# Two-layer hybrid decoder trunk: weight sums by adding transfers, and two plain blocks per feed-forward part instead of three, the second's low weight parts on GpSimd

## The chip, the cores and the metric

The kernel runs on one core of a Trainium2 chip. The core has a matrix engine (TensorE, PE in the rows; its weight loads are listed as PEld), VectorE (DVE), ScalarE (ACT), GpSimd (POOL) and SyncE (SP), which issues most transfers. Each engine works through its own queue in order and waits there for semaphores of the others. The metric is the device time of one execution in microseconds.

## The reference

Two layers on 528 tokens (16 meta tokens and 512 real ones) of width 1024, all in float32:

```python
xn = rmsnorm(h, attn_norm_g)
proj = jnp.einsum('bld,dc->blc', xn, w_in)
...
mix = jnp.concatenate([fox_out, ret_out], axis=-1)
h = h + jnp.einsum('blc,cd->bld', mix, w_out)
hn = rmsnorm(h, ffn_norm_g)
ff = jax.nn.silu(jnp.einsum('bld,df->blf', hn, w_gate)) * jnp.einsum('bld,df->blf', hn, w_up)
return h + jnp.einsum('blf,fd->bld', ff, w_down)
```

`fox_out` is causal attention of 8 heads with a forget gate, `ret_out` chunked retention of 4 heads with a group norm. The hidden width of the feed-forward part is 2816. A last norm follows, and the 16 meta tokens are dropped. The change touches the feed-forward part alone.

## The kernel before

**Numbers.** Each float32 operand of a product is split into a high and a low part (a cast on ACT, a subtraction that leaves the rest), and a product is three matmuls: high weights by high x, high by low, low by high. The split of weights is made in `convert` for plain jobs (cast at line 180, low part at 183, on GpSimd where the job has its `pool` flag, in pieces of 128 columns, else on VectorE in pieces of 512) and in `splits` for the others (cast at 888, low part at 889, always VectorE). The split of x and of activations is `split` (131 and 132).

**The feed-forward part** of a layer works on 22 blocks of 128 hidden columns, in the six rounds of `ROUNDS`. Layer 0 has 528 columns of x, in two halves of 264; layer 1 computes only the 512 real ones. x lies in eight tiles of 128 rows, k = 0 to 7.

**Plain blocks.** The first `PLAIN` blocks take gate and up as two dense products (`dense_steps`, matmuls at 206). Gate goes through `g_done` (833 or 836: scaling, then silu), up through `u_done` (844, 845, and the split of the activation into `ah`, `al`).

**Units.** The other blocks are made by `Unit`: seven products of half the depth and half the columns take the place of eight, at the price of sums of weights and of x. A unit's order on TensorE is `head` (8 chunks on plain x), `middle` (12 chunks, from `w2` and half of `w3`, on forms of x), `tail` (8 chunks), each chunk three matmuls (line 900) of 264 or 256 columns. Its weights are four jobs: `make1` splits the gate block a; `make2` makes s, whose second half is the sum of the halves of the up block b (934) and whose first half is that less a's first half (935); `make3` makes a's first half less b's first half (941); `make4` subtracts s from a's second half (947). a lies in a buffer `raw`, b in `fraw`, s in one of two buffers `S`, which the forms of x share; high and low parts lie in rings `whi`, `wlo`, `fwhi`, `fwlo` of two.

**Forms of x.** `x_forms(k)`, for k = 0 to 3, makes four sums of x's halves (861 to 865), splits them into `th` and `tl` for all units of the layer, and is placed among the steps of the plain blocks. The first unit's `middle` is the first to read them, k = 0 to 3 in turn.

**End of a unit.** `keep` copies partial results into `e` on ACT (966), `done` combines them (976 to 984) and splits the activation. The down products of a round (1035) run as `fills` between the units of the next round; a unit that has no such fill leaves its `tail` to `tails`, which is put behind the next unit's `head`.

**What sets the order.** TensorE's order is the order of the steps. The other engines' queues are ordered by a scheduler that places an instruction by its own estimate of when its inputs and buffers are there; pools give a buffer to the next tile when the last reader of the old one is done. Weights are loaded by SyncE (924 in `Unit.load`, two transfers per unit).

Of the kernel before, what the change touches and what calls it, by code (L numbers as in the profile page):

```python
# [20 lines left out]
DEPTH = 2  # L21
# [6 lines left out]
PLAIN = 3  # L28
# [11 lines left out]
def hybrid_kernel(ctx, tc, x_t, w_in, w_fl, w_out, w_gate, w_up, w_down, vecs, b_fg, rope, decay, mask, ident, out_t):  # L40
# [772 lines left out]
    def ffn(l, st, real, last):  # L813
# [40 lines left out]
        def x_forms(k):  # L854
            def go():
                if k == 0:
                    st["t"] = [[fft(f"t{p}{i}", shape=(128, 2, 4, w)) for p in "hl"] for i in range(2)]
                s = fft("S", F32, (128, 6, w), 2)
                a, b = ((h[k][:, c0:c1], h[HB + k][:, c0:c1]) for c0, c1 in HC)
                g0, g1 = vcol(V_FFN + l * NK + k), vcol(V_FFN + l * NK + HB + k)  # L860
                nc.scalar.activation(s[:, 0:2], two(h[k]), AF.Copy, scale=g0)
                nc.vector.tensor_sub(s[:, 2], s[:, 1], s[:, 0])
                for i in range(2):
                    nc.vector.scalar_tensor_tensor(s[:, 3 + i], b[1], g1, s[:, 1 + i], ALU.mult, ALU.subtract)
                nc.vector.scalar_tensor_tensor(s[:, 5], a[1], g1, s[:, 4], ALU.mult, ALU.subtract)
                th, tl = (t[:, k % 2] for t in st["t"][k // 2])
                split(th, tl, s[:, 2:6])
# [39 lines left out]
        class Unit:  # L907
# [12 lines left out]
            def load(self):  # L920
                if "a" not in self.t:
                    for n, src, pool, tag, bufs in (("a", w_gate, wp, "raw", 3), ("b", w_up, phase["ffn"], "fraw", 2)):
                        self.t[n] = pool.tile([128, NK, 128], F32, name=tag, tag=tag, bufs=bufs)
                        nc.sync.dma_start(self.t[n], src[l, self.f])

# [5 lines left out]
            def make2(self, hi, lo):  # L931
                a, b = self.t["a"], self.t["b"]
                s = self.t["s"] = fft("S", F32, (128, NK, 128), 2)
                nc.vector.tensor_add(s[:, HB:NK], b[:, 0:HB], b[:, HB:NK])
                nc.vector.tensor_sub(s[:, 0:HB], s[:, HB:NK], a[:, 0:HB])
# [3 lines left out]
            def make3(self, hi, lo):  # L939
                a, b = self.t["a"], self.t["b"]  # L940
                nc.vector.tensor_sub(b[:, 0:HB], a[:, 0:HB], b[:, 0:HB])
                splits(hi, lo, b)


            def make4(self, hi, lo):
                a, s = self.t["a"], self.t["s"]
                nc.vector.tensor_sub(a[:, HB:NK], a[:, HB:NK], s[:, 0:HB])
# [24 lines left out]
            def done(self):  # L972
# [8 lines left out]
                nc.vector.scalar_tensor_tensor(u[:, c], sg[:, c], RSC, st["R"][:, c], ALU.mult, ALU.mult)  # L981
# [67 lines left out]
        for r, (f0, f1) in enumerate(ROUNDS):  # L1049
            for f in range(f0, f1):  # L1050
                if f < PLAIN:
                    steps += dense_steps(w_gate[l, f], [(0, xs, NK, QC, g_done(f) if f else held.append)], banks=f == 1)
                    steps += dense_steps(w_up[l, f], [(0, xs, NK, QC, u_done(f))])
# [188 lines left out]

    gf = const.tile([128, NK], F32, name="gf")
# [180 lines left out]
```

## Time and profile before

| | us |
|---|---|
| median of 3 runs (lowest to highest) | 1272.61 (1271.99 to 1272.77) |
| the profiled execution | 1272.43 |
| its span | 1270.6 |
| PE busy in the span | 1253.3 |
| DVE busy | 998.6 |
| ACT busy | 687.3 |
| POOL busy | 266.9 |
| TensorE clock granted | 0.999 |

The span runs from the first to the last instruction that the profile shows; the execution takes a little more. The profile is of one execution. In rows of groups, a line of the kernel is followed by the engine, the operation, what it writes and reads, the count, the busy time in us and the mean of one in ns. In rows of the timeline, the first number is the start in us from the span's start and the second the duration; consecutive instructions of an engine overlap a little, so a start less the one before it tells how long an instruction holds its engine up. In layer 0 the first matmul of block 0 starts at 286.53, of block 1 at 298.92, of block 2 at 310.50 and of the first unit at 322.07; in layer 1 they start at 913.00, 925.41, 936.49 and 947.53.

### The profile page before, as it was taken

Reading aid. Unit: us, or ns where it says so; the run is one execution under the profiler, and the core shown is the slowest. Engines: PE = TensorE matmul, PEld = TensorE weight load, DVE = VectorE, ACT = ScalarE, POOL = GpSimd, SP = SyncE. Lnnn points to the kernel's source line nnn. Section 1 sums busy time; section 2 is a strip of 40 time slices with the busy share of each in tenths; the row PEclk is TensorE's granted clock in tenths of the full one; section 3 lists DMA queues with packets and bytes.
Section 4 is the critical chain, followed back from the end, with each engine's and each line's share of the span. In section 5 each row is a group of like instructions: output and inputs, shape, how many; then the busy total and the mean of one; then the engine's idle time right before and its main releaser. Section 6 shows DMA issues by size and latency. Waiting matters only on the chain.

```text
span 1270.6 us, 23600 instructions
## 1 busy us (share of the span) xinstructions
PE 1253.3 (99%) x9263; PEld 1195.1 (94%) x9263; DVE 998.6 (79%) x1852; ACT 687.3 (54%) x1246; POOL 266.9 (21%) x527
## 2 busy tenths in 40 slices
PE   9999999999999999999999999999999999999997
PEld 8899999999999999999998989998789999999996
DVE  8878756779888888887786877567899888888866
ACT  7666545676444444444465665456764444444444
POOL 3455545410000000000025546454100000000000
PEclk9999999999999999999999999999999999999999
DMA  6322222123233333332323232222233333333321
GB/s 217 95 71 89 87 81 83 60 68 129 92 96 100 100 100 100 100 100 84 107 70 117 61 101 83 78 90 67 100 96 121 100 100 100 100 100 100 102 81 67
DMA packets 45680, 120.57 MB, mean 95 GB/s; under 512 B 5360, under 2 KB 12272, under 8 KB 45568
## 3 DMA queue, kind: packets, MB, share of 16 engines
q1 hardware_dynamic: 45136, 118.77, 29.7%
q8 instruction: 73, 1.20, 0.4%
q14 instruction: 39, 0.32, 0.1%
q10 hardware_dynamic: 432, 0.29, 0.1%
HBM read 116.91 MB, written 2.13 MB: 94 GB/s over the span
## 4 chain that ended last, share of the span: by engine, by line
PE 93%; DVE 2%; ACT 2%; DMA 2%; issue 0%; SPq 0%; DVEq 0%; ACTq 0%
PE psd L206 29%; PE psa L900 19%; PE psd L1035 14%; PE psd L900 13%; PE psa L206 5%; PE psa L1035 4%; PE psa L407 2%; PE psa L582 2%; PE psa L497 2%; PE psa L749 1%; PE psa L719 1%; DMA bc<-cdr 1%; DMA h<-x_t 0%; DMA cdr<-z 0%; PE psa L279 0%
## 5 line engine op out<-in xcount | busy, mean ns | idle before, releaser
L183 POOL TENSOR_TENSOR wlo<-raw,whi 128x128 fp32r<-128x128 f32 x504 | 261.4, 554 | 270.0 <-ACT whi L180 250.0
L206 PE MATMUL psd<-xh,whi 128*128 128x264 f32 (+1 forms) x792 | 195.4, 314 | 0.2 <-ACT whi L180 0.2
L206 PE MATMUL psd<-xl,whi 128*128 128x264 f32 (+1 forms) x792 | 186.0, 302 | 0.5 <-DVE xl L309 0.4
L206 PE MATMUL psd<-xh,wlo 128*128 128x264 f32 (+1 forms) x792 | 186.4, 303 | 0.0
L206 PEld LDWEIGHTS psd<-xh,whi 128*128 128x128 f32 x792 | 128.0, 189 | 5.2 <-ACT whi L180 0.9
L206 PEld LDWEIGHTS psd<-xh,wlo 128*128 128x128 f32 x792 | 126.8, 188 | 6.3 <-DVE wlo L183 0.6
L206 PEld LDWEIGHTS psd<-xl,whi 128*128 128x128 f32 x792 | 127.4, 188 | 5.0 <-DVE xl L309 1.2
L180 ACT CAST whi<-raw 128x512 fp32r<-128x512 f32 (+1 forms) x168 | 98.4, 613 | 49.3 <-PE psd L206 36.4
L888 ACT CAST whi<-raw 128x1024 fp32r<-128x1024 f32 (+2 forms) x62 | 54.8, 885 | 51.3 <-PE psd L900 39.9
L888 ACT CAST fwhi<-raw 128x1024 fp32r<-128x1024 f32 (+2 forms) x62 | 55.6, 897 | 47.5 <-PE psd L900 40.0
L1135 POOL TENSOR_TENSOR th<-th,e 128x544 f32<-128x544 f32 x1 | 1.4, 1370 | 359.1 <-DVE e L1155 359.1
L85 POOL MEMSET kl<- 64x528 f32 x2 | 1.1, 534 | 345.4 <-PE psa L900 345.4
L889 DVE TENSOR_TENSOR wlo<-raw,whi 128x1024 fp32r<-128x1024 f32 (+2 forms) x62 | 62.9, 1015 | 12.8 <-ACT whi L888 12.7
L889 DVE TENSOR_TENSOR fwlo<-raw,fwhi 128x1024 fp32r<-128x1024 f32 (+2 forms) x62 | 64.0, 1032 | 10.5 <-ACT fwhi L888 10.1
L900 PE MATMUL psa<-th,whi 128*128 128x264 f32 (+1 forms) x232 | 65.4, 282 | 0.0
L900 PE MATMUL psa<-th,wlo 128*128 128x264 f32 (+1 forms) x232 | 65.4, 282 | 0.0
L900 PE MATMUL psa<-tl,whi 128*128 128x264 f32 (+1 forms) x232 | 65.3, 282 | 0.0
L900 PE MATMUL psa<-th,fwhi 128*128 128x264 f32 (+1 forms) x224 | 63.4, 283 | 0.0
L900 PE MATMUL psa<-tl,fwhi 128*128 128x264 f32 (+1 forms) x224 | 63.3, 283 | 0.0
L900 PE MATMUL psa<-th,fwlo 128*128 128x264 f32 (+1 forms) x224 | 63.3, 282 | 0.0
L517 ACT ACTIVATE pd<-pd,nmax 128x144 f32<-128x144 f32 (+1 forms) x64 | 36.9, 576 | 43.8 <-DVE nmax L504 31.8
L966 ACT COPY e<-psa 128x264 f32<-128x264 f32 (+1 forms) x114 | 42.9, 376 | 28.4 <-PE psa L900 24.1
(343 smaller groups left out, 4053.5 us busy)
## 6 DMA issues: line engine op xcount, KB each, us to landing
raw<-w_in SPq DMA_DIRECT2D x54, 512.0 KB, 3.4
raw<-w_gate SPq DMA_DIRECT2D x44, 512.0 KB, 3.8
fraw<-w_up SPq DMA_DIRECT2D x38, 512.0 KB, 3.5
raw<-w_down SPq DMA_DIRECT2D x64, 256.0 KB, 2.8
raw<-w_out SPq DMA_DIRECT2D x16, 512.0 KB, 3.4
raw<-w_down SPq DMA_DIRECT2D x32, 192.0 KB, 2.5
bc<-cdr SPq DMA_DIRECT2D x16, 264.0 KB, 3.5
raw<-w_up SPq DMA_DIRECT2D x6, 512.0 KB, 3.5
```

What stands on the lines that cost most here:

```text
L180: pin(nc.scalar.copy(hi, job["raw"][:, c0:c1]), pinned)
L183: pin(sub(lo[:, i:i + wide], job["raw"][:, c0 + i:c0 + i + wide], hi[:, i:i + wide].bitcast(F32)), pinned)
L206: nc.tensor.matmul(ps[1][b][:, 0:c1 - c0], w[:, wk, :], x[:, c0:c1], start=(k == 0 and i == 0), stop=(k == n - 1 and i == 2))
L407: nc.tensor.transpose(ps[:, 128 * j:128 * j + 128], src[:, o:o + 128], idt)
L497: nc.tensor.matmul(sc[0:nq, 0:c1 - c0], st["q"][s][:, q0:q0 + nq], kk[:, c0:c1], start=(i == 0), stop=(i == 1))
L517: nc.scalar.activation(pr, pr, AF.Exp, bias=nmax[0:nq], scale=-1.0, accum_out=rsum)
L582: nc.tensor.matmul(po[:, c0:SEQ], v[:, j, :], pp[:, j, META + c0:T], start=(j == 0 and i == 0), stop=(j == 4 and i == 1))
L888: nc.scalar.copy(hi, src)
L889: nc.vector.tensor_sub(lo, src, hi.bitcast(F32))
L900: nc.tensor.matmul(bank()[:, 0:b.shape[-1]], a[:, o + k, :], b, start=(fresh and k == 0 and i == 0), stop=(k == n - 1 and i == 2), skip_gr ...
L966: nc.scalar.copy(self.t["e"][:, i], self.t["x"][:, 0:w])
L1035: nc.tensor.matmul(v[:, 0:c1 - c0], a[:, s * n + k, :], b[:, c0:c1], start=(k == 0 and i == 0), stop=(k == n - 1 and i == 2))
```

## The change

Block 2 of each layer becomes a unit, and block 1 remains plain with its low weight parts on GpSimd (`f > 0` is the `pool` flag). The first unit then has no down product of an earlier round beside it, so its tail goes behind the next unit's head. For every unit the sum of the halves of b is made by transfers: SyncE loads the first half into s, a transfer from GpSimd's queue adds the second half to it; another adds a's first half to b's first half, again from memory. The sums at 934 and 941 go. Because a transfer can only add, some signs are turned round: the forms of x use gains of opposite sign (`ngf`, made once), two subtractions of weights become additions, and `done` scales by `-RSC`. The signs cancel in the end.

```diff
--- before.py
+++ after.py
@@ -25,7 +25,7 @@
 DFF = 2816
 NF = DFF // 128
 ROUNDS = ((0, 3), (3, 7), (7, 11), (11, 15), (15, 19), (19, 22))
-PLAIN = 3
+PLAIN = 2
 HB = NK // 2
 EPS = 1e-6
 NBLK = SEQ // 128
@@ -858,11 +858,12 @@
                 s = fft("S", F32, (128, 6, w), 2)
                 a, b = ((h[k][:, c0:c1], h[HB + k][:, c0:c1]) for c0, c1 in HC)
                 g0, g1 = vcol(V_FFN + l * NK + k), vcol(V_FFN + l * NK + HB + k)
+                n1 = ngf[:, l * HB + k:l * HB + k + 1]
                 nc.scalar.activation(s[:, 0:2], two(h[k]), AF.Copy, scale=g0)
-                nc.vector.tensor_sub(s[:, 2], s[:, 1], s[:, 0])
-                for i in range(2):
-                    nc.vector.scalar_tensor_tensor(s[:, 3 + i], b[1], g1, s[:, 1 + i], ALU.mult, ALU.subtract)
-                nc.vector.scalar_tensor_tensor(s[:, 5], a[1], g1, s[:, 4], ALU.mult, ALU.subtract)
+                nc.vector.tensor_sub(s[:, 2], s[:, 0], s[:, 1])
+                nc.vector.scalar_tensor_tensor(s[:, 3], b[1], g1, s[:, 1], ALU.mult, ALU.subtract)
+                nc.vector.scalar_tensor_tensor(s[:, 4], b[1], n1, s[:, 2], ALU.mult, ALU.subtract)
+                nc.vector.scalar_tensor_tensor(s[:, 5], a[1], n1, s[:, 4], ALU.mult, ALU.subtract)
                 th, tl = (t[:, k % 2] for t in st["t"][k // 2])
                 split(th, tl, s[:, 2:6])
             return go
@@ -922,6 +923,10 @@
                     for n, src, pool, tag, bufs in (("a", w_gate, wp, "raw", 3), ("b", w_up, phase["ffn"], "fraw", 2)):
                         self.t[n] = pool.tile([128, NK, 128], F32, name=tag, tag=tag, bufs=bufs)
                         nc.sync.dma_start(self.t[n], src[l, self.f])
+                    s = self.t["s"] = fft("S", F32, (128, NK, 128), 2)
+                    nc.sync.dma_start(s[:, HB:NK], w_up[l, self.f, :, 0:HB])
+                    nc.gpsimd.dma_start(s[:, HB:NK], w_up[l, self.f, :, HB:NK], accum_op=ALU.add)
+                    nc.gpsimd.dma_start(self.t["b"][:, 0:HB], w_gate[l, self.f, :, 0:HB], accum_op=ALU.add)
 
 
             def make1(self, hi, lo):
@@ -929,22 +934,18 @@
 
 
             def make2(self, hi, lo):
-                a, b = self.t["a"], self.t["b"]
-                s = self.t["s"] = fft("S", F32, (128, NK, 128), 2)
-                nc.vector.tensor_add(s[:, HB:NK], b[:, 0:HB], b[:, HB:NK])
-                nc.vector.tensor_sub(s[:, 0:HB], s[:, HB:NK], a[:, 0:HB])
+                a, s = self.t["a"], self.t["s"]
+                nc.vector.tensor_add(s[:, 0:HB], s[:, HB:NK], a[:, 0:HB])
                 splits(hi, lo, s)
 
 
             def make3(self, hi, lo):
-                a, b = self.t["a"], self.t["b"]
-                nc.vector.tensor_sub(b[:, 0:HB], a[:, 0:HB], b[:, 0:HB])
-                splits(hi, lo, b)
+                splits(hi, lo, self.t["b"])
 
 
             def make4(self, hi, lo):
                 a, s = self.t["a"], self.t["s"]
-                nc.vector.tensor_sub(a[:, HB:NK], a[:, HB:NK], s[:, 0:HB])
+                nc.vector.tensor_add(a[:, HB:NK], a[:, HB:NK], s[:, 0:HB])
                 splits(hi, lo, a[:, HB:NK])
 
             def bank(self, n):
@@ -978,7 +979,7 @@
                 nc.vector.scalar_tensor_tensor(sg[:, c], sg[:, c], RSC, st["R"][:, c], ALU.mult, ALU.mult)
                 silu(sg[:, c], None if self.f < NF - 1 else ROOTS if last else LOGS)
                 u = tt("tq")
-                nc.vector.scalar_tensor_tensor(u[:, c], sg[:, c], RSC, st["R"][:, c], ALU.mult, ALU.mult)
+                nc.vector.scalar_tensor_tensor(u[:, c], sg[:, c], -RSC, st["R"][:, c], ALU.mult, ALU.mult)
                 u2 = two(u)
                 nc.vector.tensor_mul(u2[:, 0], self.t["x"][:, 0:w], u2[:, 0])
                 nc.vector.tensor_mul(u2[:, 1], e[:, 2], u2[:, 1])
@@ -1049,8 +1050,8 @@
         for r, (f0, f1) in enumerate(ROUNDS):
             for f in range(f0, f1):
                 if f < PLAIN:
-                    steps += dense_steps(w_gate[l, f], [(0, xs, NK, QC, g_done(f) if f else held.append)], banks=f == 1)
-                    steps += dense_steps(w_up[l, f], [(0, xs, NK, QC, u_done(f))])
+                    steps += dense_steps(w_gate[l, f], [(0, xs, NK, QC, g_done(f) if f else held.append)], f > 0, banks=f == 1)
+                    steps += dense_steps(w_up[l, f], [(0, xs, NK, QC, u_done(f))], f > 0)
                     continue
                 u = Unit(f)
                 steps += u.head()
@@ -1240,6 +1241,10 @@
         steps.insert(4, lambda: squares(st, QC, False, False))
         return steps
 
+    ngf = const.tile([128, DEPTH * HB], F32, name="ngf")
+    for i in range(DEPTH):
+        c = V_FFN + i * NK + HB
+        nc.vector.tensor_scalar_mul(ngf[:, i * HB:i * HB + HB], vec[:, c:c + HB], -1.0)
     gf = const.tile([128, NK], F32, name="gf")
     nc.vector.tensor_scalar_mul(gf, vec[:, V_FIN:V_FIN + NK], RSC)
```

How this moves the rows of two queues is shown for the place where layer 0 goes over from plain blocks to units. Lines from 858 on shift: `x_forms` is at 862 to 866, the low parts of `splits` at 890, the sum that makes s's first half at 938, that of `make4` at 948, the loads of `Unit.load` at 925 and 927, the adding transfers at 928 (into s) and 929 (into b).

VectorE's queue before, at the end of the plain blocks of layer 0. `tl` are the low parts of the forms of x (the second one is that of k = 3), `tq` and `al` belong to an up product's activation, `sg` to a gate, `wlo<-raw` at 183 is a low part of plain weights:

```order
L132 TENSOR_TENSOR tl_4311<-S,th_4310 128x1056 [waits Activation_49]
L844 SCALAR_TENSOR_TENSOR tq<-psd,R 128x528 [waits PE_49]
L183 TENSOR_TENSOR wlo<-raw,whi 128x512 [waits DMAHW4_49,Activation_49]
L845 TENSOR_TENSOR tq<-tq,sg 128x528 [waits DVE_49]
L865 SCALAR_TENSOR_TENSOR S<-h_80,vec,S 128x264
L183 TENSOR_TENSOR wlo<-raw,whi 128x512 [waits Activation_49]
L132 TENSOR_TENSOR al_4492<-tq,ah_4491 128x528 [waits Activation_49]
L934 TENSOR_TENSOR S<-fraw 128x512 [waits DMAHW1_49]
L132 TENSOR_TENSOR tl_4311<-S,th_4310 128x1056 [waits Activation_49]
L836 SCALAR_TENSOR_TENSOR sg<-psd,R 128x528 [waits PE_49]
L889 TENSOR_TENSOR wlo<-raw,whi 128x1024 [waits DMAHW5_49,Activation_49]
L935 TENSOR_TENSOR S<-S,raw 128x512 [waits DVE_49]
```

Only the sum at 934 of the unit's own work stands ahead of the last `tl`. VectorE's queue of the change at the same place, first piece; DMAHW names a transfer of SyncE, DMASW one of GpSimd's queue, and the sum at 938 is that of the first unit:

```order
L844 SCALAR_TENSOR_TENSOR tq<-psd,R 128x528 [waits PE_49]
L865 SCALAR_TENSOR_TENSOR S<-h_79,ngf,S 128x264
L938 TENSOR_TENSOR S<-S,raw 128x512 [waits DMAHW3_49,DMASW2_49]
L866 SCALAR_TENSOR_TENSOR S<-h_79,ngf,S 128x264 [waits DVE_49]
L845 TENSOR_TENSOR tq<-tq,sg 128x528 [waits Activation_49]
L833 SCALAR_TENSOR_TENSOR sg<-psa,R 128x264 [waits DVE_49,PE_49]
L833 SCALAR_TENSOR_TENSOR sg<-psa,R 128x264 [waits PE_49]
L132 TENSOR_TENSOR al_4359<-tq,ah_4358 128x528 [waits Activation_49]
L890 TENSOR_TENSOR wlo<-raw,whi 128x1024 [waits Pool_49]
L132 TENSOR_TENSOR tl_4317<-S,th_4316 128x1056 [waits Activation_49]
L890 TENSOR_TENSOR fwlo<-S,fwhi 128x1024 [waits Activation_49]
L863 TENSOR_TENSOR S<-S 128x264 [waits Activation_49]
```

The sum at 938 waits for a transfer of GpSimd's queue and stands ahead of the low parts of the unit's first two weights. The second piece follows the first without a gap and ends with the last `tl`, that of k = 3:

```order
L844 SCALAR_TENSOR_TENSOR tq<-psd,R 128x528 [waits PE_49]
L890 TENSOR_TENSOR wlo<-fraw,whi 128x1024 [waits DMAHW1_49,DMASW0_49,Activation_49]
L845 TENSOR_TENSOR tq<-tq,sg 128x528 [waits DVE_49]
L864 SCALAR_TENSOR_TENSOR S<-h_80,vec,S 128x264
L865 SCALAR_TENSOR_TENSOR S<-h_80,ngf,S 128x264
L132 TENSOR_TENSOR al_4511<-tq,ah_4510 128x528 [waits Activation_49]
L866 SCALAR_TENSOR_TENSOR S<-h_80,ngf,S 128x264 [waits DVE_49]
L890 TENSOR_TENSOR fwlo<-raw,fwhi 128x1024 [waits DMAHW4_49]
L948 TENSOR_TENSOR raw<-raw,S 128x512 [waits DMAHW7_49]
L132 TENSOR_TENSOR tl_4317<-S,th_4316 128x1056 [waits Activation_49]
```

The activation of block 1's up (844), the low part of the third weights and that of the next unit's first weights now stand ahead of the last `tl`. GpSimd's queue at that place, as a piece of the difference; before, nothing stood there between layer 0's output projection and the start of layer 1:

```order
-L85 MEMSET kl_8415 64x528
+L929 DMA fraw<-w_gate 128x512 [waits DMAHW1_49,DMAHW0_49,DVE_49]
+L929 DMA fraw<-w_gate 128x512 [waits DMAHW2_49]
+L183 TENSOR_TENSOR wlo<-raw,whi 128x128 [waits DVE_49,PE_49,DMAHW7_49,Activation_49,Pool_49]
+L183 TENSOR_TENSOR wlo<-raw,whi 128x128 x3
+L183 TENSOR_TENSOR wlo<-raw,whi 128x128 [waits Activation_49]
+L183 TENSOR_TENSOR wlo<-raw,whi 128x128 x3
+L183 TENSOR_TENSOR wlo<-raw,whi 128x128 [waits DVE_49,PE_49,DMAHW0_49,Activation_49,Pool_49]
+L183 TENSOR_TENSOR wlo<-raw,whi 128x128 x3
+L183 TENSOR_TENSOR wlo<-raw,whi 128x128 [waits Activation_49]
+L183 TENSOR_TENSOR wlo<-raw,whi 128x128 x3
+L928 DMA S<-w_up 128x512 [waits DMAHW5_49,DVE_49]
```

The transfer that adds into the first unit's S (928) stands behind all sixteen low parts of block 1, eight of its gate and eight of its up.

## The prediction

> **What bounds the kernel now.** I read the page first, then busy times by stretch of the feed-forward parts, then the rows of one place. The page gives the span, the busy times and the chain that ended last:
>
> ```profile
> span 1270.6 us, 23600 instructions
> PE 1253.3 (99%) x9263; PEld 1195.1 (94%) x9263; DVE 998.6 (79%) x1852; ACT 687.3 (54%) x1246; POOL 266.9 (21%) x527
> PE 93%; DVE 2%; ACT 2%; DMA 2%; issue 0%; SPq 0%; DVEq 0%; ACTq 0%
> ```
>
> TensorE sets the time: 99% busy, 93% of the chain. A change gains only by taking matmuls away, and loses whatever it makes TensorE wait. VectorE's 79% is a mean, so it has to be looked at by stage. The view of busy time by stretch, over all engines, has start:end, length, then busy time and instructions of PE, weight load, DVE, ACT and POOL, the clock, DMA share and GB/s. First and third stretch are the plain blocks of layers 0 and 1, second and fourth the units:
>
> ```profile
> 286.50:322.00 35.50, 35.50 (x294) 35.35 (x293) 35.47 (x60) 22.47 (x33) 0.00 (x0) 1.00 0.34 115
> 322.00:640.00 318.00, 318.00 (x2619) 318.00 (x2619) 256.69 (x380) 144.83 (x206) 2.77 (x14) 1.00 0.33 101
> 913.00:947.00 34.00, 33.62 (x145) 26.74 (x144) 33.50 (x57) 21.33 (x32) 0.00 (x0) 1.00 0.36 120
> 947.00:1250.00 303.00, 303.00 (x2121) 283.12 (x2120) 246.78 (x358) 142.10 (x207) 0.00 (x0) 1.00 0.31 97
> ```
>
> Two things carry the prediction. In the units TensorE never idles (318.00 of 318.00, 303.00 of 303.00), so VectorE work taken away there buys nothing. In the plain blocks VectorE is as full as TensorE (35.47 of 35.50): whatever is due earlier there comes late, unless as much is taken away ahead of it.
>
> **TensorE work removed.** A plain block becomes a unit, in both layers. The same view for TensorE alone shows block 2 and the 24 matmuls of the first unit's head, layer 0 and then layer 1:
>
> ```profile
> 310.50:322.07 11.57, 11.57 (x98) 1.00 0.27 81
> 322.07:324.97 2.90, 2.90 (x27) 1.00 0.42 133
> 936.49:947.53 11.04, 11.04 (x49) 1.00 0.27 83
> 947.53:950.38 2.85, 2.85 (x25) 1.00 0.03 6
> ```
>
> A unit is 28 chunks of 3 matmuls, 84, at 2.90 / 24 = 0.1208 and 2.85 / 24 = 0.1188: 10.15 and 9.98 us. It saves 11.57 - 10.15 = 1.42 and 11.04 - 9.98 = 1.06, together **-2.5**. That is all that can be gained.
>
> **The first unit comes 11.6 us earlier.** Its head needs only plain x, its second product the four sums of x, the last of them (k = 3) as follows:
>
> ```profile
> 324.97 0.28 PE L900 MATMUL psa<-th,fwhi 128*128 128x264 f32 x1
> 326.18 0.28 PE L900 MATMUL psa<-tl,fwhi 128*128 128x264 f32 x1
> ```
>
> So `tl` of k = 3 is read 4.11 after the head begins (326.18 - 322.07). With the head at 310.50 it is wanted at 314.6, in layer 1 at 936.49 + 2.85 + 1.2 = 940.5. VectorE now works without a gap as here (start, duration):
>
> ```profile
> 311.64 0.70 DVE L844 SCALAR_TENSOR_TENSOR tq<-psd,R 128x528 f32<-128x528 f32 x1
> 312.26 0.68 DVE L183 TENSOR_TENSOR wlo<-raw,whi 128x512 fp32r<-128x512 f32 x1
> 312.86 0.70 DVE L845 TENSOR_TENSOR tq<-tq,sg 128x528 f32<-128x528 f32 x1
> 313.48 0.49 DVE L865 SCALAR_TENSOR_TENSOR S<-h,vec,S 128x264 f32<-128x264 f32 x1
> 313.88 0.69 DVE L183 TENSOR_TENSOR wlo<-raw,whi 128x512 fp32r<-128x512 f32 x1
> 314.48 0.70 DVE L132 TENSOR_TENSOR al<-tq,ah 128x528 fp32r<-128x528 f32 x1
> 315.10 0.69 DVE L934 TENSOR_TENSOR S<-fraw 128x512 f32<-128x512 f32 x1
> 315.70 1.25 DVE L132 TENSOR_TENSOR tl<-S,th 128x1056 fp32r<-128x1056 f32 x1
> 316.87 0.70 DVE L836 SCALAR_TENSOR_TENSOR sg<-psd,R 128x528 f32<-128x528 f32 x1
> 317.49 1.22 DVE L889 TENSOR_TENSOR wlo<-raw,whi 128x1024 fp32r<-128x1024 f32 x1
> 318.62 0.68 DVE L935 TENSOR_TENSOR S<-S,raw 128x512 f32<-128x512 f32 x1
> 319.22 0.68 DVE L941 TENSOR_TENSOR fraw<-raw,fraw 128x512 f32<-128x512 f32 x1
> 319.82 0.68 DVE L947 TENSOR_TENSOR raw<-raw,S 128x512 f32<-128x512 f32 x1
> 320.43 1.22 DVE L889 TENSOR_TENSOR fwlo<-S,fwhi 128x1024 fp32r<-128x1024 f32 x1
> ```
>
> `tl` of k = 3 is ready at 316.95, 2.3 too late for the new need. Starts that follow each other give what an instruction costs in the queue: 0.60 for 512 columns, 0.62 for 528, 0.40 for a half form, 1.13 for 1024, 1.17 for 1056. What is taken away up to here is eight low parts of weights and the sum at L934, 9 x 0.60 = 5.4. What comes ahead of that `tl` instead, by the new order, is the first unit's own work, until now behind it: two sums of weights and four low parts, 2 x 0.60 + 4 x 1.13 = 5.7. The ledger is even, the need 11.6 us earlier.
>
> **What VectorE does last is set by a transfer.** In the new order the sum at L938 stands ahead of everything the first unit still lacks, and waits for the transfer that adds the second half of w_up into S. From that sum to the end of `tl` of k = 3 the queue holds 20 instructions: four low parts of weights (4.52), two of x (1.17 and 1.25), five of 528 columns (3.10), two sums (1.20) and seven half forms (2.80): 14.0 us.
>
> The transfer is issued on GpSimd's queue, behind the sixteen low parts of block 1. Those of its up weights wait for a buffer that TensorE releases as it ends block 0, and for the cast on ACT:
>
> ```profile
> 298.92 0.40 PE L206 MATMUL psa<-xh,whi 128*128 128x264 f32 x2
> 299.29 1.15 ACT L180 CAST whi<-raw 128x512 fp32r<-128x512 f32 x2
> 925.87 1.13 ACT L180 CAST whi<-raw 128x512 fp32r<-128x512 f32 x2
> L183 POOL TENSOR_TENSOR wlo<-raw,whi 128x128 fp32r<-128x128 f32 x504 | 261.4, 554 | 270.0 <-ACT whi L180 250.0
> ```
>
> The first of the two casts is done at about 299.9; eight low parts by 0.554 take 4.43, to 304.3. In layer 1 it is 926.4 and 930.8. No row shows a transfer that adds, or one from GpSimd's queue; the nearest are plain ones of SyncE (median from issue to landing):
>
> ```profile
> raw<-w_down SPq DMA_DIRECT2D x64, 256.0 KB, 2.8
> fraw<-w_up SPq DMA_DIRECT2D x38, 512.0 KB, 3.5
> ```
>
> The accumulate carries 256 KB, so the lower bound is 2.8; it has to read the target and write it, at worst two transfers after one another, 7.0. I take 4.0, nearer the lower since the size is that of the first row and both reads can overlap. The Trainium skill, in "DMA: Bandwidth & Descriptors", section "Anatomy of one DMA — SWDGE (gpsimd) path", fits a transfer issued by GpSimd as about 2.0 us plus its bytes over 436 GB/s, which makes 2.6 here as an estimate and lowers each layer by 1.4, to 1286.9; no run yet shows it.
>
> Layer 0: 304.3 + 4.0 + 14.0 = 322.3 against 314.6, a stall of **7.7**. Layer 1, with 512 columns (14.0 x 512 / 528 = 13.6): 930.8 + 4.0 + 13.6 = 948.4 against 940.5, **7.9**. TensorE will not stand in one piece: the low part of the unit's first weights is late too, in its head.
>
> A floor holds whatever the transfer takes: the activation of block 1's up (L844) stands behind L938 and cannot start before that block ends, 310.50. From it to the end of that `tl` ten instructions remain, 0.62 + 1.13 + 0.62 + 0.40 + 0.40 + 0.62 + 0.40 + 1.13 + 0.60 + 1.25 = 7.2, so 317.7, 3.1 late.
>
> **A second wait.** The first unit has no down product beside it, so its tail now follows the next unit's head, and that unit's first down product reads the first unit's activation as its third block. From the end of the tail to that matmul are 36 + 12 + 2 = 50 matmuls, 50 x 0.1208 = 6.0. How long a tail's last result takes to become an activation is seen in a later unit (next matmul after the tail, and the low part of the activation):
>
> ```profile
> 441.66 0.41 PE L1035 MATMUL psd<-ah,whi 128*128 128x264 f32 x2
> 448.99 0.71 DVE L132 TENSOR_TENSOR al<-tq,ah 128x528 fp32r<-128x528 f32 x1
> ```
>
> 449.70 - 441.66 = 8.0, so TensorE waits 2.0 per layer, **4.0**. Without the weights' instructions in between it would be nothing; a fuller queue would make it 3 each.
>
> **Edits at nothing.** Two small products at the start and the flipped signs change no instruction's size. The sums taken off VectorE in the units (0.60 each) save nothing, since TensorE is full there. The additional 0.75 MB of transfers per unit lie beside work as long as they land in time: S's buffer is free when the low part two units back is done, and its sum is asked for at L935:
>
> ```profile
> 441.42 1.23 DVE L889 TENSOR_TENSOR fwlo<-S,fwhi 128x1024 fp32r<-128x1024 f32 x1 [1.80 <-ACT fwhi L888]
> 453.68 0.69 DVE L935 TENSOR_TENSOR S<-S,raw 128x512 f32<-128x512 f32 x1
> ```
>
> 442.65 plus 2.8 for the plain half is 445.5, which leaves 8.2 us for the accumulate. Up to there it costs nothing.
>
> **Sum.** 7.7 + 7.9 + 4.0 - 2.5 = +17.1: a span of 1287.7. The profiled execution took 1272.43, 1.9 more than its span of 1270.6, and the median of the runs is 1272.61, 0.2 above it; 1272.61 + 17.1 = **1289.7**. With the lower transfer, low parts at 0.43 and no second wait a layer stalls 5.5 (303.3 + 2.8 + 14.0 = 320.1) and 5.7: +8.7, 1281. With 7.0, low parts at 0.67 and 3 in each second wait it is 11.7 + 11.9 + 6 - 2.5 = +27.1, 1300. The 0.43 and 0.67 are the ends that GpSimd's rows show early in the program:
>
> ```profile
> 23.31 8.07 POOL L183 TENSOR_TENSOR wlo<-raw,whi 128x128 fp32r<-128x128 f32 x12
> 36.71 3.44 POOL L183 TENSOR_TENSOR wlo<-raw,whi 128x128 fp32r<-128x128 f32 x8 [5.22 <-ACT whi L180]
> ```
>
> **Rivals.** *Only the floor is left* (0.10): if the S sum is not last, as when the low parts of the up weights start earlier than I think, the stalls are 3.1 and 3.0, with the second wait +7.6 and 1280. Against it: S would have to land by 303.7, and the quickest rows of both parts give 303.3 + 2.8 = 306.1.
>
> *GpSimd is held up by a full VectorE* (0.12): the two groups above differ by half, on the same shape. If each low part first waits out a VectorE instruction of 0.60, eight take 8 x 1.03 = 8.2 instead of 4.43, each layer loses 3.8 more, and the time is 1297. For it: nowhere so far did GpSimd work beside a VectorE that has no gap; both plain stretches show it with 0.00. The Trainium skill says the same in "SBUF — State Buffer", section "Who interferes with whom": a VectorE instruction with two inputs in SBUF and a GpSimd instruction that reads SBUF exclude each other for a whole instruction; the 0.67 leans that way, the 0.554 of the mean only in part.
>
> *Adding transfers are slow* (0.10): at more than 8.2 us each unit waits for its S, all the way through; at 9, 38 units by 0.8 add 30, 1320. Against it: twice the 512 KB row is still only 7.0.
>
> *Faster* (0.06): VectorE has the forms in time after all, both waits vanish, and the 2.5 of TensorE remain: 1270.1. It needs the queue to reach `tl` of k = 3 some 7.7 us before the sum above says, and to be past block 1's up before it ends; the ledger speaks against it. Small stalls that just cancel the gain get 0.03.
>
> **How the numbers follow.** The forecast has 0.59. Stalls under 12 in all are rare by the floor, so the range takes the floor's case and most of GpSimd's: 1279 to 1303. Faster and no change split at 0.2%, 2.5 us, about what a measurement of this kernel can tell: 0.06 faster, 0.03 the same, 0.91 slower.
>
> **What would show it.** TensorE's idle time in one stretch behind block 1 of each layer, released by VectorE (weights' low part, e copy, `tl`), 7 to 8 us; VectorE's L938 there waiting for a transfer into S; the accumulate landing about 308; an idle of 2 us at the next unit's down product, released by `al`; none in later units. The prediction is wrong if TensorE runs through from block 1 to the units, if the first S sum never waits, or if every unit shows a gap.

## The result, and the profile after

| | us | to before, with its 95% interval |
|---|---|---|
| before, median of 4 | 1272.33 | |
| the change, median of 4 (1301.06 to 1304.26) | 1301.64 | 1.0231 (1.0217 to 1.0245) |
| span of the profiled execution, before and after | 1270.6, 1299.5 | |

The change is slower by 29.3 us; 1289.7 was forecast, with a range of 1279 to 1303. The page of the changed kernel, the lines that were shown of before, and the one on its new transfers:

```profile
span 1299.5 us, 23943 instructions
PE 1265.0 (97%) x9287; PEld 1205.8 (93%) x9287; DVE 962.4 (74%) x1780; ACT 691.3 (53%) x1252; POOL 355.3 (27%) x639
PE 85%; DVE 7%; DMA 4%; ACT 2%; issue 1%; POOL 1%; DVEq 0%; SPq 0%; ACTq 0%; POOLq 0%
S<-w_up POOLq DMA_DIRECT2D x40, 256.0 KB, 4.6
```

VectorE has 36 us less to do and now holds 7% of the chain that ended last, where it had 2%, transfers 4%. Less work, and more waiting for it: the place matters. TensorE's waits where layer 0 goes over to the units (timeline of TensorE, rows with idle time ahead of them; in brackets the idle time and what ended it):

```profile
314.78 0.59 PE L901 MATMUL psa<-xh,wlo 128*128 128x264 f32 x1 [2.93 <-DVE wlo L890]
322.73 0.39 PE L901 MATMUL psa<-th,fwhi 128*128 128x264 f32 x1 [1.13 <-ACT th L131]
324.54 0.59 PE L901 MATMUL psa<-tl,fwhi 128*128 128x264 f32 x1 [1.42 <-DVE tl L132]
...
336.01 0.39 PE L901 MATMUL psa<-th,fwlo 128*128 128x264 f32 x1 [0.47 <-DVE fwlo L890]
342.74 0.51 PE L1036 MATMUL psa<-ah,fwhi 128*128 128x264 f32 x2 [0.86 <-ACT ah L131]
344.17 0.51 PE L1036 MATMUL psa<-al,fwhi 128*128 128x264 f32 x2 [0.92 <-DVE al L132]
```

In order, TensorE waits for the low part of the first unit's first weights, the k = 3 form and its low part, the low part of the second unit's sum, and the first unit's activation at the down product. `tl` of k = 3 is read at 324.54; it was wanted at 314.6. VectorE and GpSimd in that stretch:

```profile
305.95 0.48 DVE L865 SCALAR_TENSOR_TENSOR S<-h,ngf,S 128x264 f32<-128x264 f32 x1
310.38 0.69 DVE L938 TENSOR_TENSOR S<-S,raw 128x512 f32<-128x512 f32 x1 [3.95 <-DMA S<-w_up]
...
322.63 0.68 DVE L948 TENSOR_TENSOR raw<-raw,S 128x512 f32<-128x512 f32 x1
323.23 1.25 DVE L132 TENSOR_TENSOR tl<-S,th 128x1056 fp32r<-128x1056 f32 x1
...
331.87 0.69 DVE L938 TENSOR_TENSOR S<-S,raw 128x512 f32<-128x512 f32 x1 [1.56 <-DMA S<-w_up]
```

```profile
300.64 4.88 POOL L183 TENSOR_TENSOR wlo<-raw,whi 128x128 fp32r<-128x128 f32 x8 [1.97 <-ACT whi L180]
305.47 0.87 POOL L928 DMA_DIRECT2D S<-w_up  x1
...
326.87 0.86 POOL L928 DMA_DIRECT2D S<-w_up  x1 [2.95 <-DMA S<-w_up]
329.99 0.85 POOL L928 DMA_DIRECT2D S<-w_up  x1 [2.25 <-DMA S<-w_up]
```

The first unit's transfer is issued right behind the eighth low part, at 305.47, and VectorE stands 3.95 us for it. From 310.38 to the end of `tl`, 324.48, it works for 14.1 us without a gap. The granted clock of TensorE, in pieces of 1 us (start:end, length, busy, clock), and far from that place:

```profile
313.00:314.00 1.00, 0.00 (x0) 1.00 0.00 0
316.00:317.00 1.00, 1.00 (x7) 0.50 0.00 0
328.00:329.00 1.00, 1.00 (x10) 1.00 0.89 356
400.00:650.00 250.00, 250.00 (x2056) 1.00 0.50 137
```

Behind the first idle TensorE runs at half clock, 0.22 us from one matmul to the next instead of 0.12. From 400 to 650 it never idles, as before, and no wait of TensorE shows in the later units of either layer.

In layer 0 the head of the block with f = 4 starts at 336.6 before and at 351.4 now, 14.8 later; layer 1 adds another 14. All of the loss lies behind the two plain blocks of each layer.

### The profile page after: what moved, and what is told of

Same layout as the page of the kernel before. It is cut to its first block, busy times and chain, and to the rows that moved or that the text cites. A ratio compares the mean times of both kernels' runs of the same rounds, so it can differ in the third digit from the quotient of the medians.

```text
span 1299.5 us, 23943 instructions
## 1 busy us (share of the span) xinstructions
PE 1265.0 (97%) x9287; PEld 1205.8 (93%) x9287; DVE 962.4 (74%) x1780; ACT 691.3 (53%) x1252; POOL 355.3 (27%) x639
## 4 chain that ended last, share of the span: by engine, by line
PE 85%; DVE 7%; DMA 4%; ACT 2%; issue 1%; POOL 1%; DVEq 0%; SPq 0%; ACTq 0%; POOLq 0%
PE psd L206 24%; PE psa L901 18%; PE psd L1036 14%; PE psd L901 12%; PE psa L206 4%; PE psa L1036 4%; DMA S<-w_up 2%; PE psa L407 2%; PE psa L582 2%; PE psa L497 1%; PE psa L749 1%; PE psa L719 1%; DVE fwlo L890 1%; POOL wlo L183 1%; DVE wlo L890 1%
## 5 line engine op out<-in xcount | busy, mean ns | idle before, releaser
L183 POOL TENSOR_TENSOR wlo<-raw,whi 128x128 fp32r<-128x128 f32 x536 | 280.8, 558 | 265.5 <-ACT whi L180 245.1
L206 PE MATMUL psd<-xh,whi 128*128 128x264 f32 (+1 forms) x744 | 183.0, 314 | 1.1 <-DVE sg L836 0.9
L206 PE MATMUL psd<-xh,wlo 128*128 128x264 f32 (+1 forms) x744 | 174.0, 302 | 0.0
L206 PE MATMUL psd<-xl,whi 128*128 128x264 f32 (+1 forms) x744 | 173.5, 301 | 0.4 <-DVE xl L309 0.4
L206 PEld LDWEIGHTS psd<-xh,whi 128*128 128x128 f32 x744 | 120.5, 190 | 5.9 <-issue 1.5
L206 PEld LDWEIGHTS psd<-xh,wlo 128*128 128x128 f32 x744 | 119.1, 188 | 5.6 <-DVE wlo L183 0.4
L206 PEld LDWEIGHTS psd<-xl,whi 128*128 128x128 f32 x744 | 119.7, 189 | 4.1 <-DVE xl L309 0.8
L928 POOL DMA_DIRECT2D S<-w_up x40 | 34.5, 863 | 291.7 <-DVE h L1043 249.0
L929 POOL DMA_DIRECT2D fraw<-w_gate x40 | 34.7, 871 | 254.8 <-DMA fraw<-w_up 150.5
L890 DVE TENSOR_TENSOR wlo<-raw,whi 128x1024 fp32r<-128x1024 f32 (+2 forms) x64 | 64.2, 1004 | 35.5 <-ACT whi L889 35.4
L901 PE MATMUL psa<-th,whi 128*128 128x264 f32 (+1 forms) x248 | 70.6, 285 | 0.0
```

Of the source, the lines that this page charges most:

```text
L183: pin(sub(lo[:, i:i + wide], job["raw"][:, c0 + i:c0 + i + wide], hi[:, i:i + wide].bitcast(F32)), pinned)
L206: nc.tensor.matmul(ps[1][b][:, 0:c1 - c0], w[:, wk, :], x[:, c0:c1], start=(k == 0 and i == 0), stop=(k == n - 1 and i == 2))
L890: nc.vector.tensor_sub(lo, src, hi.bitcast(F32))
L901: nc.tensor.matmul(bank()[:, 0:b.shape[-1]], a[:, o + k, :], b, start=(fresh and k == 0 and i == 0), stop=(k == n - 1 and i == 2), skip_gr ...
L928: nc.gpsimd.dma_start(s[:, HB:NK], w_up[l, self.f, :, HB:NK], accum_op=ALU.add)
L929: nc.gpsimd.dma_start(self.t["b"][:, 0:HB], w_gate[l, self.f, :, 0:HB], accum_op=ALU.add)
```

## The experiments

The theories: A, the first adding transfer comes late (behind GpSimd's low parts) and VectorE stands for it; B, every adding transfer costs; C, GpSimd working beside VectorE costs; D, VectorE simply has too much to do by the time the first unit needs it, and neither order nor transfers change that; E, the half clock costs by itself, or F, it doesn't. Ratios are to the kernel before, run beside each; 0.001 is 1.27 us.

| run | median us | ratio and interval |
|---|---|---|
| three blocks, adding transfers | 1281.03 | 1.0066 (1.0051 to 1.0081) |
| two blocks, GpSimd's low parts, no adding | 1291.0 | 1.0145 (1.0128 to 1.0162) |
| the change, first unit's sum on VectorE | 1295.96 | 1.0180 (1.0165 to 1.0195) |
| the change, idle filled with matmuls | 1301.75 | 1.0226 (1.0211 to 1.0241) |
| the change, block 1's low parts on VectorE | 1296.66 | 1.0179 (1.0164 to 1.0194) |
| the change, forms of x earlier | 1306.73 | 1.0268 (1.0251 to 1.0285) |
| no adding, forms and down product moved | 1284.03 | 1.0081 (1.0066 to 1.0096) |
| as that, more on GpSimd | 1286.81 | 1.0102 (1.0086 to 1.0117) |
| three blocks, adding from the fourth unit on | 1272.94 | 1.0005 (0.9996 to 1.0015) |
| two blocks alone | 1291.47 | 1.0152 (1.0135 to 1.0169) |
| the change, first sum and low parts on VectorE | 1294.57 | 1.0170 (1.0155 to 1.0185) |
| three blocks, adding, idle filled | 1280.83 | 1.0065 (1.0050 to 1.0080) |

### One part alone

Three plain blocks with the adding transfers (from the change: `PLAIN = 3`, and no `f > 0` at `dense_steps`).

> Three plain blocks as before, low parts of weights on VectorE as before, only the adding transfers of the change. Theory A (the loss sits where the plain blocks end, since there the first S sum is issued late; an adding transfer as such is hidden): in the changed kernel it lands 4.6 us after its issue and a unit has 8.2, so 1272 to 1274, no idle of TensorE in the units. Rival B (adding transfers cost by themselves, by their traffic or by holding VectorE and GpSimd up in each of the 38 units): 1280 or more, with idle spread over all units.

1281.03, the figure of B, but not its picture: the idle lies at the first units alone. In layer 1 one adding transfer is issued at 955.49, among loads of raw, fraw and w_down, and lands 8.0 us later. VectorE and TensorE there:

```profile
963.47 0.69 DVE L938 TENSOR_TENSOR S<-S,raw 128x512 f32<-128x512 f32 x1 [4.66 <-DMA S<-w_up]
964.08 0.68 DVE L1043 TENSOR_TENSOR h<-psd,h 128x512 f32<-128x512 f32 x1
```

```profile
964.82 0.79 PE L1036 MATMUL psd<-ah,fwhi 128*128 128x512 f32 x1 [2.91 <-DVE h L1043]
```

The sum that waits stands ahead of the addition at 1043, whose PSUM buffer TensorE needs. So I left the adding out of the first three units only (their sums on VectorE):

```diff
+                    if self.f < PLAIN + 3:
+                        return
                     s = self.t["s"] = fft("S", F32, (128, NK, 128), 2)
...
```

> Three plain blocks, adding transfers only from the fourth unit of each layer on; the first three units' sums on VectorE. With adding transfers in all units the time was 8.6 over the kernel before, and the trace shows the loss at the first units alone (2.4 in layer 0, 4.6 in layer 1, where one adding transfer took 8.0 us among other loads and VectorE stood 4.66 us at its sum). Theory A (only the first adding transfers are late): 1272 to 1274.5. Rival B (each adding transfer costs a little): 35 of 38 units are left, so 1279 or more.

1272.94, ratio 1.0005: three units of each layer are without, so 32 of the 38 (the expectation counted 35) have adding transfers, and these cost nothing that can be measured. B falls; the first units pay all.

Two plain blocks alone (all sums and low parts on VectorE), and two blocks with the second's low parts on GpSimd:

> Two plain blocks instead of three and nothing else: all sums and all low parts on VectorE. Theory D (VectorE's ledger: the first unit comes 11.6 us earlier, VectorE was full before): it has 2.4 us more ahead of the k = 3 form than the run without adding transfers (1291), which lost 6.7 us there in layer 0: 1292 to 1297. Rival C (GpSimd beside VectorE costs what it takes off): VectorE's instructions keep their size of before, 0.62 for 528 columns, and that gives the 2.4 us back: 1288 to 1292.

> Two plain blocks with the second's low parts on GpSimd, but all sums of weights on VectorE. Theory A: without the wait for a transfer the queue of VectorE runs on where it stood still for 3.95 us at 306.4; against that it has two sums more per unit, 1.2 us. TensorE's idle and its time at half clock shrink by about a third to a half in each layer: 1288 to 1294. Rival C (GpSimd working beside a full VectorE is what makes it late): that part is unchanged, so 1299 to 1303.

1291.47 (C's figure, half a us under D's) and 1291.0 (A's). Without one adding transfer two thirds of the loss are there, and moving sixteen low parts to GpSimd gains nothing. Busy times of two blocks alone (PE, weight load, DVE, ACT, POOL; then the clock, DMA share and GB/s), and VectorE's last form of x:

```profile
286.50:310.00 23.50, 23.50 (x195) 23.36 (x194) 23.46 (x43) 15.47 (x23) 0.00 (x0) 1.00 0.38 129
310.00:322.00 12.00, 6.01 (x42) 5.12 (x41) 11.96 (x18) 6.08 (x8) 0.00 (x0) 0.92 0.14 44
```

```profile
320.52 1.25 DVE L132 TENSOR_TENSOR tl<-S,th 128x1056 fp32r<-128x1056 f32 x1
```

VectorE is busy 23.46 of 23.50 and 11.96 of 12.00 us, and `tl` of k = 3 is ready at 321.77. In the run with GpSimd's low parts it is 321.17. That is D: VectorE has no wait, only work. The change, with its wait of 3.95, is at 324.48, 3.3 later than the run with GpSimd's low parts.

Why GpSimd's low parts gain nothing is read from groups of VectorE's instructions between 286 and 320 (count, busy us, mean ns), first of the change, then of two blocks alone:

```profile
L132 DVE TENSOR_TENSOR tl<-S,th 128x1056 fp32r<-128x1056 f32 x3 | 3.9, 1336 | 0.0
L863 DVE TENSOR_TENSOR S<-S 128x264 f32<-128x264 f32 x4 | 2.3, 567 | 0.0
L289 DVE SCALAR_TENSOR_TENSOR R<-nwt,R 128x528 f32<-128x528 f32 x1 | 1.0, 966 | 0.0
L836 DVE SCALAR_TENSOR_TENSOR sg<-psd,R 128x528 f32<-128x528 f32 x1 | 0.7, 696 | 0.0
```

```profile
L132 DVE TENSOR_TENSOR tl<-S,th 128x1056 fp32r<-128x1056 f32 x3 | 3.8, 1254 | 0.0
L863 DVE TENSOR_TENSOR S<-S 128x264 f32<-128x264 f32 x4 | 1.7, 427 | 0.0
L289 DVE SCALAR_TENSOR_TENSOR R<-nwt,R 128x528 f32<-128x528 f32 x1 | 0.7, 704 | 0.0
L836 DVE SCALAR_TENSOR_TENSOR sg<-psd,R 128x528 f32<-128x528 f32 x1 | 0.7, 703 | 0.0
```

Beside GpSimd the first sum of the forms (863) takes 567 ns instead of 427, the low parts of x 1336 instead of 1254, and a product of 528 columns (289) 966 instead of 704; one of the same shape with an operand in PSUM (836), which in the change starts at 304.72 and so beside GpSimd's second group of low parts, keeps its size. The change also has adding transfers, but the run without them shows the same: the four instructions of a form (863 to 866) take 558 to 638 ns there, against 427 to 490 in two blocks alone. Over the groups of that stretch the growth is about 2.2 us, and the four low parts that VectorE is spared are 2.4. C holds to that extent: what VectorE is spared it loses.

### The first transfer

Three runs on the change: the first unit's sum on VectorE, block 1's low parts on VectorE, and both.

```diff
-                    nc.gpsimd.dma_start(s[:, HB:NK], w_up[l, self.f, :, HB:NK], accum_op=ALU.add)
+                    if self.f > PLAIN:
+                        nc.gpsimd.dma_start(s[:, HB:NK], w_up[l, self.f, :, HB:NK], accum_op=ALU.add)
...
+                if self.f == PLAIN:
+                    nc.vector.tensor_add(s[:, HB:NK], s[:, HB:NK], self.t["b"][:, HB:NK])
```

> As the change, but the first unit of each layer adds the second half of w_up into S on VectorE (0.6 us) from the block it has loaded anyway. Theory A: the sum is made at 306.4 instead of 310.4, the low part of the k = 3 form is there at 306.4 + 0.6 + 14.1 = 321.1 instead of 324.5, in layer 1 the like: 6 to 8 us less, 1293 to 1296. Rival D (the ledger alone: VectorE cannot be earlier than block 1's end allows, whatever the transfer does): 318.2 in place of 321.1, 1288. Rival C (GpSimd beside VectorE): no change, 1300 to 1303.

> As the change, but the low parts of block 1's weights on VectorE as before, so that GpSimd's queue holds only the adding transfers. Theory A (the first adding transfer is late since it stands behind sixteen low parts): it is issued when its S half is loaded, and VectorE no longer waits 3.95 us for it; against that VectorE has 4 x 0.60 = 2.4 us more ahead of the unit. Some 1 to 3 us per layer are won: 1295 to 1300. Rival C (GpSimd beside VectorE is the cause): VectorE's instructions in that stretch go back to their size of before, and with the wait gone too it is more than 4 us per layer, under 1293. Rival D (VectorE's ledger alone): 2.4 us more ahead, so slower than the change, 1303 to 1307.

> As the change, with the first unit's S sum on VectorE and block 1's low parts on VectorE too; each of the two alone took 5 to 6 us off. Theory A (both act through one wait, VectorE standing for the first adding transfer): together no more than either, 1295 to 1298. Rival C (GpSimd's low parts slow VectorE by themselves, the transfer comes on top): the two add up, 1289 to 1292.

1295.96, 1296.66 and 1294.57. Each takes 5 to 6 us off and both together 7: they act through one wait, as A says, and not side by side. The traces agree. VectorE's wait of 3.95 at the first sum of layer 0 is gone, 1.05 and gone, and `tl` of k = 3 is ready at 321.84, 322.05 and 321.45, where the change has 324.48. The last time is a little under A's range and well over C's. A is right, but only for about 7 of the 29 us.

### Order

The four forms of x every 6 steps instead of every 9 (`NK + 4 + 6 * i`).

> As the change, but the four forms of x stand every 6 steps instead of every 9, so that the last one is written ahead of the first unit and not among its first steps. Theory A: in VectorE's queue the k = 3 form then has four instructions fewer ahead of it behind the wait for S (two low parts of weights and the sum for w4, 2 x 1.13 + 0.60, and more), about 4 us, so k = 3 is there at about 320.4 instead of 324.5; the wait for S itself stays: 1293 to 1298. Rival (the transfer alone decides, the order behind it doesn't matter, since the weights are wanted just as early): 1300 to 1303.

1306.73, slower, which no theory expected. `tl` of k = 3 is ready at 320.8, as reckoned. But a new wait follows, on VectorE and then TensorE:

```profile
343.47 0.69 DVE L938 TENSOR_TENSOR S<-S,raw 128x512 f32<-128x512 f32 x1 [2.82 <-DMA S<-w_up]
344.08 0.70 DVE L132 TENSOR_TENSOR al<-tq,ah 128x528 fp32r<-128x528 f32 x1
```

```profile
344.84 0.81 PE L1036 MATMUL psa<-al,fwhi 128*128 128x264 f32 x2 [2.96 <-DVE al L132]
```

The fourth unit's transfer, issued at 337.20, lands 6.2 us later, and its sum now stands ahead of the activation that the down product needs. Without adding transfers, the same earlier forms and the first down product one unit later (`if fills and f > PLAIN + 1`):

> As the run without adding transfers, with two changes of order: the forms of x every 6 steps, and the first down product moved from beside the second unit to beside the third. It had lost 6.7 us by the last form of x and 1 to 2 at the down product in each layer, and 1.5 to 2 at half clock. Theory A (three separate lateness: S's transfer, the place of the forms, the down product that comes too early): with all three gone VectorE's sums and low parts for the first two units remain, 2 to 4 us per layer: 1276 to 1281. Rival D (VectorE's ledger is what counts, order only shifts it): 1287 to 1291.

1284.03, between the two. VectorE in layer 0, and TensorE:

```profile
313.26 1.25 DVE L132 TENSOR_TENSOR tl<-S,th 128x1056 fp32r<-128x1056 f32 x1
...
318.09 1.22 DVE L890 TENSOR_TENSOR fwlo<-S,fwhi 128x1024 fp32r<-128x1024 f32 x1
```

```profile
318.08 0.39 PE L901 MATMUL psa<-th,fwhi 128*128 128x264 f32 x1 [1.75 <-ACT fwhi L889]
```

The form is now in time, at 314.51, and the low part of the second weights, whose cast TensorE waits for, comes at 318 to 319 instead. Layer 0 still loses 7.5, half clock included (the first block of layer 1 starts at 920.53, before at 913.00). Order chooses what is late, as D says; in its strict form, in which order changes nothing, D falls too, since 7 of the 18.6 us over before went by order alone.

Then more of VectorE's work went to GpSimd (low parts of block 0 and of the first unit's first weights, with `True` for `f > 0` and a `pool` argument in `splits`), with the first unit's sums ahead of other work and the forms every 5 steps.

> As the run before, with VectorE relieved where the first unit starts: the low parts of block 0, of block 1 and of the first unit's first weights all on GpSimd, the first unit's sums ahead of other work on VectorE, the forms of x every 5 steps. Theory A together with the ledger: TensorE runs through from the plain blocks to the units but for about 1 us, and the 2.5 us of matmuls saved show: 1270 to 1273. Rival C (GpSimd beside a full VectorE holds it up): GpSimd works on without a gap from 280 to 310, so 1278 or more.

1286.81, no better, as C had it. GpSimd's low parts of the first unit's first weights, and TensorE, which at block 1's up waits for a PSUM buffer that VectorE still reads:

```profile
312.54 8.42 POOL L892 TENSOR_TENSOR wlo<-raw,whi 128x128 fp32r<-128x128 f32 x8
```

```profile
308.36 0.48 PE L206 MATMUL psd<-xh,whi 128*128 128x264 f32 x2 [3.39 <-DVE sg L836]
```

A low part takes 8.42 / 8 = 1.05 us there, against 0.61 in the change (4.88 / 8). VectorE was nearly full beside both (7.73 of 8.50 and 4.87 of 4.90 us), so that alone doesn't explain the difference; its cause stays open.

### The half clock

The idle of the change at the k = 3 form was filled with matmuls on old operands (28 in layer 0, 40 in layer 1), into a bank that the next product overwrites:

```diff
...
+                        nc.tensor.matmul(y()[:, 0:w], ones, x_block(0, 0)(0)[0], start=True, stop=True)
```

> As the change, with 28 (layer 0) and 40 (layer 1) matmuls more on old operands, whose result is overwritten, put where TensorE waits for the k = 3 form of x. Theory E (an idle of some us halves the granted clock for the next 3 to 6 us, and that is what the prediction left out): the idle is filled, the clock stays at 1.00 after 324.5 and 965.4, and 1.7 + 2.0 us that were lost there come back: 1297 to 1299. Rival F (the half clock costs nothing, since the matmuls it slows would have waited anyway): 1301 to 1303.

1301.75: behind k = 3 the clock is now 1.00 (326 to 338), and no time comes back. Over both places where the layers go over to units, TensorE was at half clock for 23.9 us in the change and for 6.8 in this run. From the first unit's head to that of the block with f = 4 it took 38.9 us instead of 39.9 in layer 0 (312.38 to 351.27), but 38.7 instead of 38.4 in layer 1 (952.16 to 990.90). TensorE reaches the second unit earlier, counted from the first, and waits there, behind the second adding transfer (and runs at half clock behind that wait, from 338 to about 341):

```profile
335.48 0.39 PE L901 MATMUL psa<-th,fwhi 128*128 128x264 f32 x1 [0.61 <-ACT fwhi L889]
337.38 0.39 PE L901 MATMUL psa<-th,fwlo 128*128 128x264 f32 x1 [1.40 <-DVE fwlo L890]
```

```profile
333.61 0.69 DVE L938 TENSOR_TENSOR S<-S,raw 128x512 f32<-128x512 f32 x1 [3.71 <-DMA S<-w_up]
```

The same with three blocks and adding transfers, where one idle stood alone (24 matmuls into a bank that nobody reads, ahead of that down product):

> As the run with three plain blocks and adding transfers in all units, with 24 matmuls more, whose result nobody reads, put in layer 1 where TensorE stood idle for 2.91 us at a down product and then ran at half clock for some 3 us, with no other wait behind it. Theory E (an idle of about 3 us halves the clock, and where no later wait swallows it that is lost): the clock stays at 1.00 and 1.6 us come back, 1278.5 to 1280. Rival F: no difference in what follows, 1281 or, if the matmuls run over the idle, more.

1280.83 against 1281.03: nothing again. TensorE's next waits in that execution:

```profile
966.25 0.50 PE L1036 MATMUL psd<-ah,fwhi 128*128 128x512 f32 x1 [0.33 <-DVE h L1043]
972.55 0.38 PE L901 MATMUL psa<-th,whi 128*128 128x256 f32 x1 [1.13 <-ACT e L967]
```

The first is what is left of the old idle; the second isn't in the run without filling, where the clock was at half for 3.4 us. But ACT's copy, for which TensorE waits at 972.55, stands behind the cast of `ah` here and ahead of it there, so a new order in ACT's queue has its part, and the 1.6 us that E expected is less than the interval of such a run is wide. It is the first filling that speaks: E's 3.7 us did not come back, with 17 us less of half clock. F stands for this place: TensorE follows VectorE and ACT there, and half clock mostly spends time that it would have waited; up to 1 us in a layer may be its own. An idle without anything late behind it was not tried.

No version with two blocks came near the kernel before. The best, 1284.03, is 0.8% over it, and the one version level with it is three blocks with the transfers where they change nothing.

## Why the prediction held, and where it was off

**Direction and place held.** Slower, by waits of TensorE right behind the plain blocks of each layer and at the second unit's down product, released by VectorE and by ACT's casts behind it; none in later units; VectorE's first sum waiting for a transfer. All that stands in the rows above. The time is within the range, near its upper end, and that is partly luck: the range was wide for a slower transfer, slower low parts and a longer second wait, while most of what was missed came from elsewhere, as follows.

**TensorE work removed.** 2.5 us by the same windows. The units run through as before (250.00 of 250.00), so nothing contradicts it; it was not measured by itself.

**The stall at k = 3** was put at 7.7 and 7.9. In layer 0 it is 324.54 - 314.6 = 9.9, in layer 1 about 10.1, counted in the same way. The 14.0 us of VectorE's queue behind the sum were 14.1. Two terms ahead of it were small: the low parts ended at 305.5 instead of 304.3 (the cast began 0.6 later, and they took 0.61 each, not 0.554), and the transfer took 4.9 (305.47 to 310.38), not 4.0. These terms make up the 2.2. It was not all idle time, though, as the prediction had it (7 to 8 us): TensorE idled 5.5 us in layer 0 (2.93 + 1.13 + 1.42) and 7.1 in layer 1. In layer 0, 0.95 more went by block 1's end (311.45 instead of 310.50) and the rest by matmuls at half clock.

**What follows it** was put at 2.0 per layer, the second wait. That wait was 1.8 to 1.9 (0.86 + 0.92 in layer 0) but not alone: layer 0 lost 14.8 + 1.4 - 9.9 = 6.3 behind k = 3, layer 1 some 4.9. The rest is the second unit's weights, and matmuls at half clock, about 1.6 at a time by their pitch. The second unit's S lies in the first unit's buffer, which the first unit's last sum (948) holds until 323.31. Only then is it loaded (at 323.34); the adding transfer follows at 326.87, and VectorE waits 1.56 for it at 331.87. The third unit's S lies in the buffer of the k = 3 form and is loaded from 324.51; its sum waits 0.84 at 334.12, ahead of the low part of the second unit's sum that TensorE wants at 336.01. The filled idle says that weights and half clock are mostly one loss and not two: at full clock TensorE waits longer for that second unit. The prediction had no term for either; 4.3 + 2.9 us were missed here and 2.2 + 2.2 at k = 3, together 11.6 of the 12.2 between 17.1 and 29.3.

**The cause was named too narrowly.** The prediction said that what VectorE does last is set by a transfer, and gave a floor of 3.1 per layer for everything else, from block 1's end. The runs show the reverse weights. Two plain blocks alone cost 1.0152, about 19 us, with no adding transfer; VectorE was busy 35.4 of 35.5 us on the way, and `tl` of k = 3 was 7.2 late (321.77). The floor failed since it asked only when the last activation may start and not whether VectorE would be there; the ledger (5.4 taken away, 5.7 added, need 11.6 earlier) had the answer and was used only as a remark. The transfer added 3.3 at k = 3, and with the later ones about 10 us in all.

**The rivals.** Only the floor left: refuted, by the run without adding transfers (1291, not 1280). GpSimd held up: in part; its low parts took 0.61, not 1.03 (1.05 only in the run with more on GpSimd), and what it cost was VectorE's time. Slow adding transfers in each unit: refuted by the run from the fourth unit on. Transfers of 6 to 8 us do occur: up to 6.7 in later units of the change, where no sum waits for them, and 8.0 among the loads of the first units, where there was no 8.2 us of slack to begin with. Faster: refuted.

## What to carry to other kernels

Before an engine's work is made due earlier, add up what the engine that feeds it has to do until then: if it is full, moving single instructions, their order or one transfer mostly changes what is late. A load that an in-order engine waits for delays everything queued behind, so a sum may move to a transfer only where its buffer comes free a transfer's worst time ahead (8 us here, not the median of 4.6): steady units had that, the first units did not. Idle and half clock of an engine that follows another need not be two losses; fill the idle and see if time comes back.

## What the runs showed of the hardware

Around an idle of about 3 us (2.93 at 314.78) the granted clock fell to 0.50. In the change it was there from 314.2 to 321.0, 324.4 to 327.8 and 344.9 to 348.3 in layer 0, 955.9 to 959.3 and 962.7 to 969.5 in layer 1, so each time for 3.4 us or for 6.8. Idles of 1.13 and 1.42 with single matmuls between them did the same, while the pair of 1.00 and 0.92 in layer 1 (at 983 to 985) did not, nor did an idle of 3.05 in the filled run (at 315.84). The Trainium skill, "TensorE: Matmul & The Clock Gate", section "Part 1: The HAM clock gate (the "warmup" mystery)", gives half rate after an idle window of about 3.4 us and full rate after a busy one, with windows that run freely; these stretches of one and of two such windows, and like idles with and without a fall, fit that. None of the idles of the change lasted 3.4 us (the longest was 2.94), so here a window with some work in it was enough; how much work keeps the clock up was not measured.

An adding transfer of 256 KB from GpSimd's queue took 4.6 us in the median, where plain ones of SyncE to the same buffer took 2.6 (both in the changed kernel), 0.86 us of it on GpSimd; among other loads up to 8.0.

VectorE slows beside GpSimd only in some instructions: 966 instead of 704 ns for a product of 528 columns with both operands in SBUF, 696 and 703 for one of that shape with one of them in PSUM. The Trainium skill states this in "SBUF — State Buffer", section "Who interferes with whom": a VectorE instruction with two inputs in SBUF and a GpSimd instruction that reads SBUF exclude each other, one with a single input there is not touched. These rows agree.
